# First matrix memory of a hybrid encoder layer: two of four key blocks turned by VectorE and DRAM, mask sums on VectorE, units in one written order

## The chip, the cores and the metric

The kernel runs on one core of one Trainium2 chip. The metric is the device time of one execution in microseconds (us); lower is better. A core has TensorE (PE: matmuls and turns, written to eight PSUM banks), VectorE (DVE), ScalarE (ACT), GpSimd (POOL) and SyncE (SP). DMAs are issued from queues of SP and POOL. Each engine works through its own list of instructions in order and waits on semaphores.

## The reference

One encoder layer over two sequences of 512 tokens, model width 1024: a half-step SwiGLU FFN, a mixing block, a second half-step FFN, a final norm. The mixing block runs grouped-query attention and a bidirectional matrix memory (mLSTM) side by side on one projection `w_in`. What the change touches is the memory: four heads of width 128, for each head and direction

```
D    = b[:, None] - b[None, :] + li[None, :]          # b: running sum of log forget gates, li: input gate
S_qk = (q @ k.T) * exp(D - m)                         # masked to the past (forward) or the future (backward)
h    = (S_qk @ v + ...) / max(|sum S_qk + ...|, exp(-m))
...
h = h_fwd + h_bwd                                     # then RMS norm per head, times head_norm
mem = sigmoid(o_pre) * h
...
merged = sigmoid(g_att) * (att @ w_up_att) + sigmoid(g_mlstm) * (mem @ w_up_mlstm)
x = x + merged @ w_out
```

All is float32.

## The kernel before, in words

Activations lie transposed, channels on partitions and 512 tokens along the row. A float32 product is made of three float32r products: each operand is split into a high part (ACT copy) and a low part (DVE subtraction; `split`, lines 733 and 734, and for weights lines 284 and 285). So a projection of 128 output channels from 1024 inputs is 24 matmuls of 512 columns, one from 512 inputs (the merges) is 12.

`mix(s, ...)` is the mixing block of sequence s. The two sequences' blocks are generators that are run in turns. Work is written as *units*, pairs of a weight load and its matmuls; `go` runs them with one unit's load ahead for s = 0 (two for s = 1). A weight used by both sequences is loaded and split in s = 0 and parked in DRAM (line 309), and only fetched again in s = 1. Units here: `mem_values` (four units of 24 matmuls), `mem_qk(h, j)` (queries or keys of a head), `att_gate(d)`, `mem_gate(d)` (24 matmuls each), `merge_att(d)`, `merge_mem(d)` (12 each).

The order of instructions on each engine is made by a planner: a list scheduler that goes by priority (the order in which things are written, shifted by `with shifted(n)`) and by a model of durations and landing times. `pin` puts an instruction behind the one written just before it on its engine; `mark(i, last)` pins only while `marks[0]` is true.

The memory of a head (`mem_head`, line 1299) makes for each of four query blocks i a 128 x 512 score product in PSUM (line 1309), decay weights by `exp` on ACT (line 1323) from two rows that DMA spreads over the partitions (`mem_rows`: line 1088, and line 1091 adds the mask), the product of both on DVE (line 1325), and joins both directions in one 128 x 512 tile `Ts[i][0]` (lines 1336 to 1339). Since the value product needs keys on partitions, every 128 x 128 block of it must be turned.

In s = 0 `mem_out` (line 1359) turns all four key blocks j on PE: four turns (line 1372) into a PSUM bank, a split, and three value matmuls into one bank (line 1381). Then come the square (line 1390), the gate product, block sums, the root and the norm (lines 1391 to 1399). The heads stand in the loop at line 1423; the planner is free to order the units around them.

In s = 1 no PE turns are made: `mem_blocks` turns 32 x 32 blocks on DVE (line 1347), `mem_send` writes them to DRAM through POOL's queue (line 1355), and `mem_out` fetches them whole (line 1368). Its units are written out in one order with pins (lines 1401 to 1422).

Row tiles of 128 x 512 come from pools: `t2` (eleven), `f2` (four). Weight buffers: four `w8`. PSUM: three banks `mm`, one `o`, two `s`, two `t`. `mg` holds the gate rows, 128 x 8 x 512; rows 4 to 7 hold the raw queries until attention has turned them, rows 6 and 7 then stand empty until `att_gate(6)` and `att_gate(7)`.

Of the kernel before, what the change touches and what calls it, by code (L numbers as in the profile page):

```python
# [8 lines left out]
F32 = mybir.dt.float32  # L9
# [3 lines left out]
ALU = mybir.AluOpType  # L13
# [13 lines left out]
def encoder(ctx, tc, I, outs):  # L27
# [32 lines left out]
    def T2(dtype=F32, tag="t2"):  # L60
        if tag in ("eb", "ac"):
            i = boxes[tag]
            boxes[tag] += 1
            return boxes["tile"][:, i % 4 + (4 if tag == "ac" else 0), :]
        if tag == "R":
            return spool.tile([P, S], dtype, tag="R", bufs=2, name=nm("R"))
        n = {"t2": 11, "f2": 4}[tag]
        return tpool.tile([P, S], dtype, tag=tag, bufs=n, name=nm(tag))
# [723 lines left out]
    def go(*units):  # L792
        for load, comp in units:
            held.append((comp, load()))
            while len(held) > ahead[0]:
                c, w = held.pop(0)
                c(w)
# [67 lines left out]
    def mix(s, xh, xl, early=None, extra=None, after=None):  # L865
# [5 lines left out]
        def fill(n):  # L871
            go(*queue[:n])
            del queue[:n]

        def F2(dtype=F32):
            return T2(dtype, "f2")
# [145 lines left out]
        def mem_values():  # L1022
            def done(pvv):
                vm = A([P, 2, 4, S], F32R, "Vm")
                for b in range(4):
                    nc.scalar.activation(vm[:, 0, b, :], pvv[b], AF.Copy, scale=rcol(b))
                    rest(vm[:, 1, b, :], pvv[b], b, f(vm[:, 0, b, :]))
                Vm.append(vm)
            return tok_proj(xh, xl, [(1792, 512)], 2, done, (MM, MM, MM, PO))
# [27 lines left out]
        def att_gate(d):  # L1057
            def done(pp):
                gate_of(mg[:, d, :], pp)
            return win_cols(2832 + d * P, done)  # L1060
# [23 lines left out]
        def mem_rows(h, d):  # L1084

            eb = T2(F32, "eb")
            eb3 = eb.rearrange("p (b s) -> p b s", b=4)
            nc.sync.dma_start(eb3, ebuf[d, :, h, :].partition_broadcast(P))
            em = T2(F32, "eb")
            em3 = em.rearrange("p (b s) -> p b s", b=4)  # L1090
            (V_ if s or not h else G_).tensor_tensor(em3, eb3, tabs[3][:, d].unsqueeze(1).to_broadcast([P, 4, P]), op=ALU.add)
            return eb3, em3

        def mem_scales():
# [178 lines left out]
        def merge_att(d):  # L1273
            def done(pu):
                V_.scalar_tensor_tensor(mg[:, d, :], mg[:, d, :], 1.0, pu, op0=ALU.add, op1=ALU.mult)
            return up_unit(0, d, att, done)
# [17 lines left out]
            return up_unit(1, d, mem, done, (PS, PT)[d % 2])  # L1294

        mem = A([P, HM, 2, S], F32R, "mem")
        own = [T2(F32, "R")] if s else []

        def mem_head(h):
            qk = qks[h]  # L1300
            ebs, ems = zip(*[mem_rows(h, d) for d in range(2)])
            dn_ = small(8, "dn")
            dn = dn_.rearrange("p (d b) -> p d b", d=2)
            Ts = []
            for i in range(4):
                p = PS()
                isl = slice(i * P, (i + 1) * P)
                for n, (a, b) in enumerate(((0, 2), (0, 3), (1, 2))):
                    nc.tensor.matmul(p, qk[a][:, isl], qk[b], start=(n == 0), stop=(n == 2))
                pair = []  # L1310
                for d in range(2):
                    W = T2()
                    st_ = i if d == 0 else 3 - i
                    for j in range(st_ + 1):
                        b = j if d == 0 else 3 - j
                        if j == st_:
                            src, bias = ems[d][:, j], bd[:, d, st_, h:h + 1]
                        else:
                            src = ebs[d][:, j]
                            dist = st_ - j  # L1320
                            bias = (n1[:, d, st_, h:h + 1] if dist == 1 else
                                    n2[:, d, st_, h:h + 1] if dist == 2 else n2[:, d, 1, h:h + 1])
                        nc.scalar.activation(W[:, b * P:(b + 1) * P], src, AF.Exp, bias=bias)
                    cl = slice(0, (i + 1) * P) if d == 0 else slice(i * P, S)
                    V_.scalar_tensor_tensor(W[:, cl], p[:, cl], DM ** -0.5, W[:, cl], op0=ALU.mult, op1=ALU.mult,
                                            accum_out=dn[:, d, st_:st_ + 1])
                    pair.append(W)
                Ts.append(pair)
            V_.scalar_tensor_tensor(dn_, dn_, -1.0, dn_, op0=ALU.mult, op1=ALU.max)
            V_.tensor_tensor(dn, dn, en[:, :, :, h], op=ALU.max)  # L1330
            V_.reciprocal(dn_, dn_)
            for i in range(4):
                tf, tb = Ts[i]
                rf, rb = dn[:, 0, i:i + 1], dn[:, 1, 3 - i:4 - i]
                lo_, di_, up_ = slice(0, (i + 1) * P), slice(i * P, (i + 1) * P), slice((i + 1) * P, S)
                nc.scalar.activation(tf[:, lo_], tf[:, lo_], AF.Copy, scale=rf)
                V_.scalar_tensor_tensor(tf[:, di_], tb[:, di_], rb, tf[:, di_], op0=ALU.mult, op1=ALU.add)
                if i < 3:
                    V_.tensor_scalar(tf[:, up_], tb[:, up_], rb, None, op0=ALU.mult)
            return Ts  # L1340
# [18 lines left out]
        def mem_out(h, Ts):  # L1359
            moved = isinstance(Ts, int)  # L1360
            vm = Vm[0]
            po = PO()
            hs_ = slice(h * P, (h + 1) * P)
            turned = []
            for j in range(4 + 1):
                if j < 4 and moved:
                    p = F2()
                    mark(nc.gpsimd.dma_start(p, tbuf[Ts][4 * j:4 * j + 4].rearrange("c r a x -> (c r) (a x)")), True)
                elif j < 4:
                    p = PT()  # L1370
                    for i in range(4):
                        nc.tensor.transpose(p[:, i * P:(i + 1) * P], Ts[i][0][:, j * P:(j + 1) * P], ident)
                if j < 4:
                    ph, pl = T2(F32R), T2(F32R)
                    split(p, ph, pl)
                    turned.append((j, ph, pl))
                if j >= 1:
                    t, ph, pl = turned.pop(0)
                    with shifted(15):
                        for n, (a, b) in enumerate(((0, ph), (1, ph), (0, pl))):  # L1380
                            mark(nc.tensor.matmul(po, vm[:, a, t, hs_], b, start=(t == 0 and n == 0),  # L1381
                                                  stop=(t == 3 and n == 2)), True)
            h2 = T2()
            og = ogs[h]
            if moved:
                rows_ = T2()
                nc.scalar.activation(rows_.rearrange("p (i a m) -> p i a m", i=4, a=4),
                                     po.rearrange("p (a i m) -> p i a m", i=4, a=4), AF.Copy)
                po = rows_
            nc.scalar.activation(h2, po, AF.Square)  # L1390
            V_.scalar_tensor_tensor(og, og, 1.0, po, op0=ALU.add, op1=ALU.mult)
            turned_ = own[0] if own else F2()
            row = block_sums(h2, turned_)
            with shifted(60):
                rh = block_rstd(row, DM)
            with shifted(160):
                Rh = spread_rows(rh, turned_)
                V_.scalar_tensor_tensor(og, og, hn[:, h:h + 1], Rh, op0=ALU.mult, op1=ALU.mult)
                split(og, mem[:, h, 0, :], mem[:, h, 1, :])

        if s:
# [18 lines left out]
            go(*[mem_gate(d) for d in range(EARLY)])  # L1420
            mem_out(3, at[3])
            marks[0] = False
        for h in range(HM if not s else 0):
            Ts = mem_head(h)
            if h == 0:
                go(*mem_values())
            queue.append(merge_att(2 * h))
            if h == 0:
                queue.append(merge_att(1))
            fill(1 + s)  # L1430
            mem_out(h, Ts)
            if h + 2 < HM:
                queue.extend([att_gate(h + 6), mem_qk(h + 2, 0), mem_qk(h + 2, 1)])
            if h:
                queue.append(merge_att(2 * h + 1))
            fill(99)

        mh, ml = A([P, KD, S], F32R, "mh"), A([P, KD, S], F32R, "ml")
        go(*[mem_gate(d) for d in range(EARLY * s, KD)])
        go(*[merge_mem(d) for d in range(KD)])  # L1440
        flush()
        yield None
# [553 lines left out]
```

## Time and profile before

| what | before |
|---|---|
| time, median of 3 runs | 2029.29 us (2028.79 to 2030.15) |
| profiled execution | 2029.24 us, span 2027.5 us |
| PE busy | 2015.1 us (99%) |
| DVE busy | 1592.6 us (79%) |
| ACT busy | 919.2 us (45%) |
| POOL busy | 249.7 us (12%) |
| granted clock of PE | 0.999 |

The span runs from the first to the last instruction; the time of the execution is 1.7 us longer. Busy time is that of the named engine. Names such as `pst<-ident,t` say what is written (a bank of pool `t`) from what (`ident` and a row tile). Three numbers with slashes are least, median and largest duration in ns. A bracket at the end of a row of the timeline is idle time of that engine just before it, and what ended it.

### The profile page before, as it was taken

To read this page: it belongs to the slowest core of one execution; us is meant where nothing else is said; L and a number is where in the kernel's file an instruction comes from. 1 tells how busy PE (TensorE), PEld (TensorE's weight loads), DVE (VectorE), ACT (ScalarE), POOL (GpSimd) and SP (SyncE) were. 2 spreads that over 40 slices of the span, in tenths; PEclk is the share of its full clock that TensorE was granted. 3 is DMA by queue.
4 is the path that set the end of the run, shared out by engine and by line. 5 is a ranking of instruction groups with operands and counts; after the bars stand their busy time and mean duration, and the time that the engine had idled before them with its cause. 6 is when DMAs were issued, how large, how long until landed. Compare 5 with 4: busy or idle time off the path is not lost.

```text
span 2027.5 us, 26874 instructions
## 1 busy us (share of the span) xinstructions
PE 2015.1 (99%) x9129; PEld 1661.4 (82%) x9129; DVE 1592.6 (79%) x2830; ACT 919.2 (45%) x1677; POOL 249.7 (12%) x313
## 2 busy tenths in 40 slices
PE   9999999999999999999999999999999999999998
PEld 7888888888888888788888878888888888888887
DVE  8989898896688788786566867377798988786797
ACT  7644444443224477653325655245444444442224
POOL 0243344201003000100120023011000000000001
PEclk9999999999999999999999999999999999999999
DMA  9778787799766766868657668867565655699753
GB/s 313 233 235 271 228 279 244 258 337 373 264 220 220 274 194 198 267 206 300 210 165 220 205 228 264 274 208 238 157 210 171 226 168 178 204 339 349 272 194 120
DMA packets 329546, 482.11 MB, mean 238 GB/s; under 512 B 23016, under 2 KB 196160, under 8 KB 328128
## 3 DMA queue, kind: packets, MB, share of 16 engines
q1 hardware_dynamic: 316352, 439.27, 64.9%
q0 software_dynamic: 12896, 40.86, 5.9%
q8 instruction: 72, 1.18, 0.2%
q14 instruction: 66, 0.54, 0.1%
q10 hardware_dynamic: 160, 0.27, 0.0%
HBM read 308.70 MB, written 171.61 MB: 237 GB/s over the span
## 4 chain that ended last, share of the span: by engine, by line
PE 94%; DVE 2%; DMA 2%; issue 1%; ACT 1%; SPq 0%; DVEq 0%; ACTq 0%
PE mm L856 16%; PE mm L380 11%; PE pso L380 11%; PE pst L380 11%; PE mm L650 9%; PE mm L842 5%; PE pss L380 5%; PE pss L650 4%; PE pst L650 4%; PE mm L821 3%; PE pso L650 3%; PE pss L1118 1%; PE pso L1165 1%; PE pso L1381 1%; PE pst L856 1%; PE pss L856 1%
## 5 line engine op out<-in xcount | busy, mean ns | idle before, releaser
L380 PE MATMUL pst<-xc,w 128*128 128x512 f32 x1056 | 253.8, 389 | 0.5 <-ACT t L415 0.5
L380 PEld LDWEIGHTS pst<-xc,w 128*128 128x128 f32 x1056 | 198.1, 188 | 42.0 <-ACT t L415 0.9
L380 PE MATMUL mm<-xc,w 128*128 128x512 f32 x972 | 229.8, 390 | 0.8 <-ACT t L388 0.8
L380 PEld LDWEIGHTS mm<-xc,w 128*128 128x128 f32 x972 | 181.8, 188 | 39.5 <-ACT t L388 1.9
L650 PE MATMUL mm<-rt,w 128*128 128x512 f32 x765 | 178.7, 389 | 0.0
L856 PE MATMUL mm<-xh,w 128*128 128x512 f32 x560 | 176.0, 391 | 0.0
L650 PEld LDWEIGHTS mm<-rt,w 128*128 128x128 f32 x765 | 143.5, 188 | 29.8
L338 ACT ACTIVATE w<-t 128x512 fp32r<-128x512 f32 x176 | 107.6, 628 | 130.7 <-issue 59.1
L339 DVE TENSOR_TENSOR w<-t,w 128x512 fp32r<-128x512 f32 x176 | 120.2, 701 | 31.7 <-ACT w L338 30.0
L380 PE MATMUL pso<-xc,f 128*128 128x512 f32 x528 | 127.1, 390 | 0.1
L380 PE MATMUL pss<-xc,w 128*128 128x512 f32 x528 | 126.8, 389 | 0.0
L380 PE MATMUL pso<-xc,w 128*128 128x512 f32 x528 | 126.8, 389 | 0.0
L856 PEld LDWEIGHTS mm<-xh,w 128*128 128x128 f32 x560 | 104.9, 188 | 21.8
L380 PEld LDWEIGHTS pso<-xc,f 128*128 128x128 f32 x528 | 98.9, 188 | 21.5 <-DVE t L419 1.1
L380 PEld LDWEIGHTS pss<-xc,w 128*128 128x128 f32 x528 | 99.1, 188 | 20.6
L380 PEld LDWEIGHTS pso<-xc,w 128*128 128x128 f32 x528 | 99.1, 188 | 20.6
L842 PE MATMUL mm<-xh,w 128*128 128x512 f32 x336 | 110.5, 395 | 0.0
L856 PE MATMUL mm<-xl,w 128*128 128x512 f32 x280 | 109.6, 391 | 0.0
L733 ACT ACTIVATE w<-wr 128x512 fp32r<-128x512 f32 x72 | 45.1, 632 | 138.3 <-PE pso L650 70.6
L733 ACT ACTIVATE w<-t 128x512 fp32r<-128x512 f32 x82 | 51.8, 632 | 107.4 <-PE pst L650 62.4
L650 PE MATMUL pss<-rt,w 128*128 128x512 f32 x396 | 93.7, 389 | 0.0
L650 PE MATMUL pst<-rt,w 128*128 128x512 f32 x396 | 93.7, 389 | 0.0
(464 smaller groups left out, 4168.1 us busy)
## 6 DMA issues: line engine op xcount, KB each, us to landing
rt<-rbuf SPq DMA_DIRECT2D x154, 512.0 KB, 5.8
w<-wpark SPq DMA_DIRECT2D x112, 512.0 KB, 5.1
wpark<-w SPq DMA_DIRECT2D x64, 512.0 KB, 3.6
wr<-in_ffn_w_gate_dram SPq DMA_DIRECT2D x62, 512.0 KB, 5.5
wr<-in_ffn_w_up_dram SPq DMA_DIRECT2D x44, 512.0 KB, 4.8
rbuf<-f SPq DMA_DIRECT2D x86, 256.0 KB, 4.3
rbuf<-R SPq DMA_DIRECT2D x82, 256.0 KB, 4.7
rbuf<-tab SPq DMA_DIRECT2D x74, 256.0 KB, 3.9
```

The source lines that it names most:

```text
L338: pin(nc.scalar.activation(t[:, 0], src, AF.Copy))
L339: pin(V_.tensor_tensor(t[:, 1], src, f(t[:, 0]), op=ALU.subtract))
L380: nc.tensor.matmul(p, a[:, k, :], xt[:, b, k, :], start=(first and k == 0 and i == 0), stop=(k == HK_ - 1 and i == 2), skip_group_check=True)
L650: nc.tensor.matmul(p, u[:, a, d * P:(d + 1) * P], r[:, b, ts], start=(first and q == 0 and k == 0), stop=(q == len(us) - 1 and k == 2), sk ...
L733: nc.scalar.activation(hi, src, AF.Copy)
L821: mark(nc.tensor.matmul(p[b][:, :N], a[:, k, bs], w_[:, kl, :], start=(k == 0 and i == 0), stop=(k == KD - 1 and i == 2)), (kl, b, i) == ( ...
L842: pin(nc.tensor.matmul(p[0], a[:, k, :], b, start=(k == 0 and i == 0), stop=(k == n - 1 and i == 2)))
L856: mark(nc.tensor.matmul(p, a[:, k, :], b, start=(k == 0 and i == 0), stop=last), last)
L1118: pin(nc.tensor.matmul(p, qT[:, h, b * P:(b + 1) * P], kv[:, hk * 2 + j, :], start=(j == 0), stop=(j == 1)))
L1165: pin(nc.tensor.matmul(pos[h], Vst[:, kb, h // 4, :], w, start=(kb == KBS[0] and i == 0), stop=(kb == KBS[3] and i == 1)))
L1381: mark(nc.tensor.matmul(po, vm[:, a, t, hs_], b, start=(t == 0 and n == 0), stop=(t == 3 and n == 2)), True)
```

## The change

In s = 0, key blocks 0 and 1 of each head are turned by DVE in 32 x 32 blocks (four instructions of 128 x 256 a head) into rows 6 and 7 of `mg`, sent to DRAM in four DMAs on POOL's queue and fetched back in two. Key blocks 2 and 3 are turned on PE as before, and now stand first in the value product. The value product's columns come in another order, so that an ACT copy puts them back (as in s = 1). The mask sums of heads 1 to 3 move from POOL to DVE. The units around the four heads are written out in one order, and the last matmul of each, the turns, the value matmuls and the DMAs are pinned; five of the `mem_gate` units are written among the heads, where before all eight stood behind them. The norm uses the copied row as its scratch row. The counts of matmuls, units and weight loads stay.

```
-            (V_ if s or not h else G_).tensor_tensor(em3, eb3, tabs[3][:, d]...)
+            V_.tensor_tensor(em3, eb3, tabs[3][:, d]...)
...
+        def half_send(h, Ts):
+            q = mg[:, 6:8].rearrange("p a (n i m) -> p (a n) i m", i=4, m=32)
+            for i in range(4):
+                V_.transpose(q[:, :, i, :], Ts[i][0][:, 0:256].rearrange("p (n m) -> p n m", m=32))
+            for a in range(4):
+                mark(nc.gpsimd.dma_start(tbuf[h % 2][0:8, :, a, :].rearrange("n r x -> r n x"),
+                                         q[32 * a:32 * a + 32].rearrange("r n i m -> r n (i m)")), True)
+        def half_turns(h, Ts):
+            got = []
+            for j in (2, 3):
+                p = PT()
+                for i in range(4):
+                    mark(nc.tensor.transpose(p[:, i * P:(i + 1) * P], Ts[i][0][:, j * P:(j + 1) * P], ident), True)
+                got.append((j, *parts(p.rearrange("p (i a m) -> p a i m", i=4, a=4))))
+            return got
+        def half_values(h, po, got):
+            for t, ph, pl in got:
+                for n, (a, b) in enumerate(((0, ph), (1, ph), (0, pl))):
+                    mark(nc.tensor.matmul(po, Vm[0][:, a, t, h * P:(h + 1) * P], b, ...), True)
+        def half_rest(h):
+            got = []
+            for j in range(2):
+                p = F2()
+                mark(nc.gpsimd.dma_start(p, tbuf[h % 2][4 * j:4 * j + 4].rearrange("c r a x -> (c r) (a x)")), True)
+                got.append((j, *parts(p)))
+            return got
+        def half_norm(h, po):
...
-        for h in range(HM if not s else 0):
-            Ts = mem_head(h)
-            if h == 0:
-                go(*mem_values())
-            queue.append(merge_att(2 * h))
-            if h == 0:
-                queue.append(merge_att(1))
-            fill(1 + s)
-            mem_out(h, Ts)
-            if h + 2 < HM:
-                queue.extend([att_gate(h + 6), mem_qk(h + 2, 0), mem_qk(h + 2, 1)])
-            if h:
-                queue.append(merge_att(2 * h + 1))
-            fill(99)
+        else:
+            qk2, qk3 = [[mem_qk(h, j) for j in range(2)] for h in (2, 3)]
+            ma = [merge_att(d) for d in range(KD)]
+            mgs = [mem_gate(d) for d in range(KD)]
+            marks[0] = True
+            for h, (first, one, more) in enumerate((
+                    ([*mem_values(), qk2[0]], qk2[1], [ma[0], ma[1], ma[2]]),
+                    ([ma[3], qk3[0], qk3[1]], ma[4], [ma[5], mgs[0]]),
+                    ([mgs[1]], mgs[2], [att_gate(6)]),
+                    ([att_gate(7), ma[6]], ma[7], [mgs[3], mgs[4]]))):
+                Ts = mem_head(h)
+                half_send(h, Ts)
+                go(*first)
+                got = half_turns(h, Ts)
+                go(one)
+                po = PO()
+                half_values(h, po, got)
+                go(*more)
+                half_values(h, po, half_rest(h))
+                half_norm(h, po)
+            marks[0] = False
...
-        go(*[mem_gate(d) for d in range(EARLY * s, KD)])
+        go(*([mem_gate(d) for d in range(EARLY, KD)] if s else mgs[5:]))
```

Since `go` runs one unit behind, the last unit of each list computes at the start of the next list.

More of the change, by code (lines that the diff above doesn't have):

```diff
@@ L1090, in mem_rows @@
             em3 = em.rearrange("p (b s) -> p b s", b=4)
-            (V_ if s or not h else G_).tensor_tensor(em3, eb3, tabs[3][:, d].unsqueeze(1).to_broadcast([P, 4, P]), op=ALU.add)
+            V_.tensor_tensor(em3, eb3, tabs[3][:, d].unsqueeze(1).to_broadcast([P, 4, P]), op=ALU.add)
             return eb3, em3
@@ L1296, in mix @@
         mem = A([P, HM, 2, S], F32R, "mem")
-        own = [T2(F32, "R")] if s else []
+        own = T2(F32, "R") if s else None
         def mem_head(h):
@@ L1391, in mem_out @@
             V_.scalar_tensor_tensor(og, og, 1.0, po, op0=ALU.add, op1=ALU.mult)
-            turned_ = own[0] if own else F2()
+            turned_ = own if s else po
+            row = block_sums(h2, turned_)
+            with shifted(60):
+                rh = block_rstd(row, DM)
+            with shifted(160):
+                Rh = spread_rows(rh, turned_)
+                V_.scalar_tensor_tensor(og, og, hn[:, h:h + 1], Rh, op0=ALU.mult, op1=ALU.mult)
+                split(og, mem[:, h, 0, :], mem[:, h, 1, :])
@@ new lines, in half_values @@
+        def half_values(h, po, got):
+            for t, ph, pl in got:
+                for n, (a, b) in enumerate(((0, ph), (1, ph), (0, pl))):
+                    mark(nc.tensor.matmul(po, Vm[0][:, a, t, h * P:(h + 1) * P], b, start=(t == 2 and n == 0),
+                                          stop=(t == 1 and n == 2)), True)
+        def half_rest(h):
[5 more added lines that the diff above has]
+            return got
@@ new lines, in half_norm @@
+        def half_norm(h, po):
+            h2 = T2()
+            og = ogs[h]
+            if True:
+                rows_ = T2()
+                nc.scalar.activation(rows_.rearrange("p (i a m) -> p i a m", i=4, a=4),
+                                     po.rearrange("p (a i m) -> p i a m", i=4, a=4), AF.Copy)
+                po = rows_
+            nc.scalar.activation(h2, po, AF.Square)
+            V_.scalar_tensor_tensor(og, og, 1.0, po, op0=ALU.add, op1=ALU.mult)
+            turned_ = own if s else po
```

## Prediction

> **What bounds the kernel now.** I read the engine shares first, then the busy time by stage, then the chain of waits inside the stage that the change touches.
>
> ```profile
> span 2027.5 us, 26874 instructions
> ...
> PE 2015.1 (99%) x9129; PEld 1661.4 (82%) x9129; DVE 1592.6 (79%) x2830; ACT 919.2 (45%) x1677; POOL 249.7 (12%) x313
> ```
>
> TensorE (PE) is busy for 2015.1 of 2027.5 us, so time is won only by giving PE less to do or by closing its few gaps. The stages, with columns PE, PEld, DVE, ACT, POOL, granted clock, DMA share and GB/s:
>
> ```profile
> 797.00:960.00 163.00, 161.90 (x750) 131.20 (x749) 122.06 (x271) 89.65 (x182) 8.66 (x7) 1.00 0.75 253
> 960.00:1160.00 200.00, 200.00 (x962) 166.52 (x962) 138.13 (x290) 93.55 (x187) 28.48 (x42) 1.00 0.62 195
> 1160.00:1300.00 140.00, 139.26 (x617) 112.78 (x616) 89.69 (x257) 66.31 (x161) 29.45 (x52) 1.00 0.78 259
> ```
>
> The first row holds the first matrix memory (s = 0), the last row the second one (s = 1), which already turns all its blocks through VectorE (DVE) and DRAM. PE idles 1.10 us in the first and 0.74 us in the second. Next, the operation that the change halves, and two rows of the chain of waits that price it:
>
> ```profile
> L1372 PE MATMUL pst<-ident,t x64: 270/272/328, 828.3 to 916.2; 128*128 128x128 f32 x64
> ...
> 828.50 0.87 PE pst L1372 x8
> ...
> 834.27 5.89 PE mm L856 x26
> ```
>
> All 64 turns of L1372 lie in s = 0 (16 a head). One is in flight for 272 ns, but on the chain, where matmuls overlap, eight take 0.87 us: 0.109 us each. A 512-column matmul takes 5.89/26 = 0.227 us there. The 1.10 us of idle time are these two gaps (the bracket is idle time and its releaser):
>
> ```profile
> 812.54 0.97 PE L1309 MATMUL pss<-qk 128*128 128x512 f32 x3 [0.70 <-DVE t L1325]
> ...
> 854.72 0.93 PE L1309 MATMUL pss<-qk 128*128 128x512 f32 x3 [0.40 <-DVE t L1325]
> ```
>
> **The change part by part.**
>
> *Half of the PE turns go.* Four heads lose 8 turns each: 32 × 0.109 = **3.5 us** off the chain. PE gets nothing new: units, scores and value matmuls are the same, in another order. The Trainium skill ("TensorE: Matmul & The Clock Gate", Part 4: PE-mode transpose) puts a turn at about 275 ns in a kernel's context. By that the term would be 8.8 us; the trace has that duration in flight, but 0.109 us a turn on the chain, and I take the chain.
>
> *Block turns on DVE, sends and fetches on GpSimd's queue (POOL).* The prices stand in s = 1:
>
> ```profile
> L1347 DVE STREAM_TRANSPOSE qt<-t x32: 407/411/444, 1191.0 to 1261.9; 128x256 f32<-128x256 f32 x32
> 1239.86 2.73 DVE L1347 STREAM_TRANSPOSE qt<-t 128x256 f32<-128x256 f32 x8
> L1355 POOL DMA_DIRECT2D tbuf<-qt x32: 582/585/618, 1194.2 to 1266.3; - x32
> DMA to landing us min/median/max: 3.8/5.9/7.1
> 1242.56 4.64 POOL L1355 DMA_DIRECT2D tbuf<-qt  x8 [17.50 <-DVE qt L1347]
> 1248.70 1.12 POOL L1368 DMA_DIRECT2D f<-tbuf  x2 [1.50 <-DMA tbuf<-qt]
> L1368 POOL DMA_DIRECT2D f<-tbuf x16: 537/546/572, 1203.0 to 1272.6; - x16
> DMA to landing us min/median/max: 3.0/5.8/9.1
> L1387 ACT ACTIVATE t<-pso x4: 597/598/601, 1225.9 to 1297.1; 128x512 f32<-128x512 f32 x4
> ```
>
> DVE: 16 turns × 2.73/8 = 5.5 us. ScalarE (ACT): four row copies as at L1387, 4 × 0.60 = 2.4 us. POOL: 16 sends × 0.585 and 8 fetches × 0.546 = 13.7 us. DMA: 16 × 128 KB and 8 × 256 KB, some 4 MB beside the 253 GB/s × 163 us = 41 MB that the stage moves, share 0.75 to about 0.83. The splits of the two fetched blocks cost as before, but read SBUF instead of PSUM (ACT 622 for 596 ns, DVE 691 both times):
>
> ```profile
> L733 ACT ACTIVATE t<-pst x50: 575/596/602, 726.3 to 1171.9; 128x512 fp32r<-128x512 f32 x50
> L733 ACT ACTIVATE t<-f x46: 615/622/633, 730.9 to 1294.6; 128x512 fp32r<-128x512 f32 x46
> L734 DVE TENSOR_TENSOR t<-pst,t x50: 652/691/694, 727.0 to 1172.6; 128x512 fp32r<-128x512 f32 x50
> L734 DVE TENSOR_TENSOR t<-f,t x46: 659/691/701, 731.6 to 1295.5; 128x512 fp32r<-128x512 f32 x46
> ```
>
> *The six mask sums of heads 1 to 3 move from POOL to DVE.*
>
> ```profile
> L1091 POOL TENSOR_TENSOR box<-box,tab x6: 1285/1294/1734, 819.3 to 880.6; 128x512 f32<-128x512 f32 x6
> L1091 DVE TENSOR_TENSOR box<-box,tab x1: 684/684/684, 803.3 to 803.3; 128x512 f32<-128x512 f32 x1
> ...
> 849.97 3.04 POOL L1091 TENSOR_TENSOR box<-box,tab 128x512 f32<-128x512 f32 x2 [13.33 <-DMA box<-ebuf]
> 852.12 1.98 DVE L285 TENSOR_TENSOR w<-wr,w 128x1024 fp32r<-128x1024 f32 x1
> 856.78 1.23 DVE L285 TENSOR_TENSOR w<-wr,w 128x1024 fp32r<-128x1024 f32 x1
> ```
>
> DVE gains 6 × 0.68 = 4.1 us and POOL loses 7.7 us. But DVE pays already: while POOL ran two sums at 849.97, a weight split on DVE took 1.98 instead of 1.23 us. It ran just ahead of the 0.40 us gap at 854.72; with these sums on DVE I count that gap closed, **0.4 us** (0 to 0.4). The 0.70 us at 812.54 belongs to head 0, whose sums were on DVE already: it stays. DVE ends at 122.06 + 5.5 + 4.1 = 132 of 163 us, ACT at 92: neither becomes the bound on average.
>
> *The wait that is new.* The value matmuls of the two fetched blocks are pinned behind the units written before them, and can go only when the data are back. From the last finished score row: four turns 1.4 us; four sends until the first fetch may go 6.1 (1242.56 to 1248.70); the second fetch's issue 0.55; its landing 5.8 (3.0 to 9.1); split on ACT and DVE 0.62 + 0.69. Sum 15.2 us (12.4 to 18.5). On PE, between a head's own turns and those matmuls, in units of 24 matmuls (5.4 us) or 12 (2.7 us):
> - head 0: 8 turns 0.9, qk 5.4, six value matmuls 1.4, qk 5.4, two merges 5.4: 18.5 us;
> - heads 1 and 2: 0.9 + 5.4 + 1.4 + 5.4 = 13.1 us, and 2.7 more where the next head's scores slip in;
> - head 3: 0.9 + 2.7 + 1.4 + 2.7 + 5.4 = 13.1 us.
>
> So head 0 is covered and the others are short by 2.1 us if their scores are finished only when the turns start. How far ahead they are is read from head 2 of before:
>
> ```profile
> 882.39 1.36 PE pss L1309 x6
> ...
> 893.28 0.68 PE pst L1372 x6
> ```
>
> A head's scores take 10.9 us to be ready. Heads 1 and 3 have 10.9 us of units and 2.7 us of scores ahead of their turns, so they are about 2.7 us early, and that pays for the 2.1. Head 2 has one gate unit, 8.2 us with the scores: 2.7 us late, unless its scores start under head 1's last units. Unpinned matmuls of later units can fill such holes, as far as three PSUM banks and the weight buffers reach. Lower end 0; upper end three heads at 5.4 us (18.5 - 13.1) plus 2.7: 19 us. The nearest row is the 0.74 us of the whole s = 1 stage, but with longer cover; I take **1.3 us**. The Trainium skill ("DMA: Bandwidth & Descriptors", Anatomy of one DMA) gives about 2.0 us + bytes/436e3 for a DMA of this kind. An estimate by it is 2.3 us for a send, 2.6 us for a fetch, and no wait at all; the landings measured here are 5.9 and 5.8 us, and they decide.
>
> *Queues.* The send and fetch are in written order on POOL. A fetch that waits 6 us holds up only the next head's sends, which come later anyway; without the mask sums nothing else stands there. The six sums now wait for their DMA in DVE's queue, and the fetched blocks' splits in ACT's. What such a wait costs s = 1 (us in total, times, longest):
>
> ```profile
> DVE box L1091 <- DMA box<-ebuf: 5.9, 3, 2.9
> ACT t L733 <- DMA f<-abuf: 5.3, 1, 5.3
> ...
> 851.01 1.05 ACT L284 ACTIVATE w<-wr 128x1024 fp32r<-128x1024 f32 x1
> 919.50 0.60 ACT L1390 ACTIVATE t<-pso 128x512 f32<-128x512 f32 x1 [2.05 <-PE pso L1381]
> 928.98 0.63 ACT L733 ACTIVATE mem<-box 128x512 fp32r<-128x512 f32 x1 [3.44 <-DVE box L1398]
> ```
>
> Behind them stand weight splits (L284: 1.05 us on ACT, L285: 1.23 us on DVE a unit). A unit's weights are split while the unit before runs, 5.4 us, so 5.4 - 2.3 = 3.1 us are spare; waits of up to 2.9 us are hidden, one of 5.3 us costs PE 2.2 us. That lies in the bounds above. SP's loads and parked stores follow the units' order at unchanged count: nothing. Gate rows 6 and 7 hold the turned blocks until head 3's sends are read, so att_gate(6)'s result stays in its PSUM bank some 8 us longer; two banks held, the third serves the merge: hidden. Five mem gates come earlier and hold five of eleven row tiles; the last four, 21.8 us, still hide head 3's norm, about 10 us (919.50 to 929.61, the last two rows).
>
> **The sum.** -3.5 - 0.4 + 1.3 = -2.6 us. The profiled execution took 2029.24 us around its span of 2027.5 (1.7 us outside), 0.05 us under the median of 2029.29. So 2029.24 - 2.6 = **2026.6 us**, a change of 0.13%.
>
> **The rivals.**
> - *Clean cover:* no new wait, and the small waits of values on split turns shrink too. For it: head 0 is fully covered, and unpinned units can fill. Against: 13.1 us against 15.2. Time: 2029.24 - 3.5 - 1.1 = 2024.6, 2023.5 with the transitions.
> - *A turn is worth its whole 272 ns:* 32 × 0.272 = 8.7 us, 2020.5 us. Against: eight in 0.87 us. The skill's Part 4 stands beside this one.
> - *The gain is eaten:* two heads short by 2.1 us each (4.2), or one stalled split (2.2) and one head: 2029.24 - 3.9 + 4.2 = 2029.5 us; up to 2033 with three. The change then takes turns off PE as it says, and gives the time back as waits at the value matmuls.
> - *Slower:* the round trip through DRAM at its long end, 18.5 us, in heads 1 to 3. Each is then 5.4 us short, less what slips in (2.7 in two): 10.8 us; 2029.24 - 3.9 + 10.8 = 2036 us. It decides from 2.7 us a head on (3 × 2.7 = 8.0 = 3.9 + 4.1). For it: the DMA share goes above 0.8, landings reached 9.1 us. Against: unpinned work for the holes.
>
> **How the numbers follow.** 0.2% of 2029 is 4.06 us, about what a measurement can tell from no change: under 2025.2 is faster, over 2033.3 slower. Chances: forecast (2025.2 to 2028.5) 48%, clean cover 20%, a full 272 ns 2%, eaten (2028.5 to 2033.3) 18%, slower 12%. Faster 0.22, same 0.66, slower 0.12. The range from 2023.5 to 2032.3 leaves out the 272 ns case, most of the slower case and the edge of the eaten one.
>
> **What the profile after would show.** Right: L1372's 64 turns gone, 32 in their place; 16 more block turns on DVE; no mask sum on POOL; PE idle in the stage near 2 us; the stage some 3 us shorter with everything behind it shifted. Wrong: value matmuls of blocks 0 and 1 idling on a split or on the fetch, a weight split late behind a waiting ACT or DVE, or a merge waiting for a bank held by the gate rows.

## The result, and the profile after

| what | before | after |
|---|---|---|
| median of 5 runs each, same chip | 2029.29 us (2028.58 to 2031.49) | 2048.78 us (2047.93 to 2050.12) |
| ratio, 95% interval | | 1.0094 (1.008 to 1.0109) |
| span of the profiled execution | 2027.5 us | 2046.3 us |

The change costs 19.5 us, 0.96%. The forecast of 2026.6 us missed on size and on sign, and the range ended at 2032.3. The page of the changed kernel, its span and engine shares:

```profile
span 2046.3 us, 26875 instructions
...
PE 2018.2 (99%) x9097; PEld 1662.3 (81%) x9097; DVE 1597.9 (78%) x2852; ACT 922.6 (45%) x1681; POOL 256.0 (13%) x331
```

The span grew by 18.8 us, and two subtractions split that. PE's idle time went from 2027.5 - 2015.1 = 12.4 to 2046.3 - 2018.2 = 28.1 us: **15.7 us more waiting**. Its busy time went up by 3.1 us although 32 turns are gone (9129 to 9097 instructions), which should have taken off 3.5: so the matmuls that are left took about **6.6 us more** (an estimate, as the 3.5 us are the prediction's term). Both lie in the stage of the first matrix memory (columns as before: PE, PEld, DVE, ACT, POOL, granted clock, DMA share, GB/s):

```profile
797.00:960.00 163.00, 145.86 (x622) 115.48 (x621) 113.10 (x266) 84.63 (x173) 13.89 (x24) 0.93 0.76 248
```

PE is busy for 145.86 of 163 us, where it was 161.90; the granted clock is 0.93, where it was 1.00. What PE waited for there (total, times, longest, in us), and the waits in PE's timeline:

```profile
PE pst L1415 <- DVE t L1339: 6.6, 1, 6.6
PE pso L1422 <- ACT t L733: 4.9, 2, 3.2
PE mm L856 <- DVE mg L889: 3.4, 1, 3.4
```
```profile
877.62 1.22 PE L1422 MATMUL pso<-t,Vm 128*128 128x512 f32 x2 [3.21 <-ACT t L733]
...
914.69 0.73 PE L1422 MATMUL pso<-t,Vm 128*128 128x512 f32 x2 [1.65 <-ACT t L733]
...
931.37 0.74 PE L1415 MATMUL pst<-ident,t 128*128 128x128 f32 x2 [6.64 <-DVE t L1339]
932.94 1.54 PE L1415 MATMUL pst<-ident,t 128*128 128x128 f32 x6 [0.83 <-DVE t L1337]
934.32 2.93 PE L1422 MATMUL pso<-t,Vm 128*128 128x512 f32 x6
940.61 5.14 PE L856 MATMUL mm<-att,w 128*128 128x512 f32 x12 [3.37 <-DVE mg L889]
```

Three kinds of wait are new. L1422 waits for the split of a fetched block (heads 1 and 2). The first turns of head 3 (L1415; L1372 in the kernel before) wait 6.64 us for its score rows, not for its own trip through DRAM. A merge (L856) waits 3.37 us for a bank that the multiplication of a gate result (L889) still holds. The granted clock falls at the long ones; each row gives its mean over 5 us:

```profile
875.00:880.00 5.00, 2.38 (x6) 1.90 (x7) 2.40 (x4) 2.10 (x3) 0.00 (x0) 0.70 0.75 265
880.00:885.00 5.00, 5.00 (x16) 3.91 (x15) 0.78 (x3) 0.76 (x2) 0.00 (x0) 0.62 0.79 261
...
915.00:920.00 5.00, 5.00 (x23) 3.94 (x21) 3.02 (x7) 3.13 (x9) 0.00 (x0) 1.00 0.93 317
...
930.00:935.00 5.00, 2.80 (x10) 2.01 (x10) 4.79 (x16) 3.00 (x6) 0.55 (x1) 0.50 1.03 313
935.00:940.00 5.00, 2.25 (x6) 1.28 (x4) 0.83 (x2) 0.12 (x1) 1.81 (x4) 0.50 0.69 205
940.00:945.00 5.00, 4.39 (x10) 3.47 (x11) 3.17 (x5) 1.23 (x2) 1.12 (x2) 0.50 0.36 108
```

Behind the gap of 3.21 us a matmul takes 0.43 us (the chain below, 878.84); in stretches of 2.5 us the clock is 0.50 from 877.5 to 882.5. The second slow stretch begins within the gap of 6.64 us and stays at 0.50 from 930 to 945. The gap of 3.37 us lies inside it, and the twelve merge matmuls behind that gap take 5.14 us, where the prediction counted 2.7. The gap of 1.65 us leaves the clock at 1.00.

Why the waits arise shows in two views. First the chain of waits, cut to the turns and the round trip of head 1 and to the passage from head 2 to head 3:

```profile
861.11 0.23 DVE t L1337
861.34 1.02 DVE mg L1405 x3
...
862.65 1.35 POOL tbuf L1407 x3
...
864.41 5.12 DMA tbuf<-mg
...
870.16 6.76 DMA f<-tbuf
876.94 0.64 ACT t L733
877.62 1.22 PE pso L1422 x2
878.84 0.43 PE pss L1309
...
917.30 0.61 ACT t L1438
917.96 0.50 issue
918.47 2.19 ACT t L1323 x8
```

From the end of the last score row (861.11 + 0.23 = 861.34) to the value matmul at 877.62 the round trip takes 16.3 us; the prediction had 15.2. At the passage from head 2 to head 3, head 3's first decay weights (L1323) run straight behind head 2's copy (L1438) and square (L1441). ACT's timeline shows this for heads 1 and 3:

```profile
848.51 0.63 ACT L1441 ACTIVATE t<-t 128x512 f32<-128x512 f32 x1
849.04 5.07 ACT L1323 ACTIVATE t<-box,st 128x128 f32<-128x128 f32 x17
...
917.93 0.63 ACT L1441 ACTIVATE t<-t 128x512 f32<-128x512 f32 x1
918.47 5.66 ACT L1323 ACTIVATE t<-box,st 128x128 f32<-128x128 f32 x19
...
928.90 0.40 ACT L1323 ACTIVATE t<-box,st 128x128 f32<-128x128 f32 x1 [2.88 <-DVE box L1449]
```

L1441 is the square in a head's norm, behind its last value matmul. Head 3 needs twenty weights, and the last of them waits until L1449, the last multiplication of head 2's norm, is done. No input of a weight comes from there. That the norm's copied row, read by L1449, holds the row tile which the last weight needs fits both the trace and the program, but no run isolates it.

So a head's decay weights begin only when the head before has its fetched blocks back, and at head 3 the last one waits for the whole norm. (Two of head 3's four score products were made on PE earlier, at 904.27; they had to wait for their weights.) The hypothesis from this: neither the round trip nor the order of the heads costs anything alone, but **in series** a head needs its weights and scores, then the trip, then the copy, and only then the next head's weights start. The units that PE has for one head are shorter than that chain.

### The profile page after: what moved, and what is told of

It reads as the page before. It is cut to its first block, busy times and chain, and to the rows that moved or that the text cites. A ratio compares the mean times of both kernels' runs of the same rounds, so it can differ in the third digit from the quotient of the medians.

```text
span 2046.3 us, 26875 instructions
## 1 busy us (share of the span) xinstructions
PE 2018.2 (99%) x9097; PEld 1662.3 (81%) x9097; DVE 1597.9 (78%) x2852; ACT 922.6 (45%) x1681; POOL 256.0 (13%) x331
## 4 chain that ended last, share of the span: by engine, by line
PE 92%; DMA 3%; DVE 2%; ACT 2%; issue 1%; POOL 0%; SPq 0%; DVEq 0%; ACTq 0%; POOLq 0%
PE mm L856 14%; PE pso L380 12%; PE pst L380 11%; PE mm L380 10%; PE mm L650 8%; PE pss L380 6%; PE mm L842 5%; PE pss L650 4%; PE pst L650 4%; PE mm L821 3%; PE pso L650 3%; PE pss L1118 1%; PE pso L1165 1%; PE pst L856 1%; PE pss L856 1%; PE pso L821 1%
## 5 line engine op out<-in xcount | busy, mean ns | idle before, releaser
L856 PE MATMUL mm<-xh,w 128*128 128x512 f32 x560 | 177.5, 392 | 0.0
L856 PEld LDWEIGHTS mm<-xh,w 128*128 128x128 f32 x560 | 105.4, 188 | 22.1
L856 PE MATMUL mm<-xl,w 128*128 128x512 f32 x280 | 109.8, 392 | 0.0
```

Source lines behind the costliest of these rows:

```text
L856: mark(nc.tensor.matmul(p, a[:, k, :], b, start=(k == 0 and i == 0), stop=last), last)
```

## The experiments

Each ran beside runs of the kernel before on the same chip; ratios are to those.

**Written order without the trip** (`pe_turns`). All four blocks are turned on PE; order, pins and DVE's mask sums are those of after.

```
-                half_send(h, Ts)
                 go(*first)
...
-                half_values(h, po, half_rest(h))
+                half_values(h, po, half_turns(h, Ts, (0, 1)))
```

> Keeps the changed kernel's written order, pins and DVE mask sums, but turns all four key blocks on PE; blocks 0 and 1 are turned where the fetch stood. No block turns, sends or fetches in s = 0. Theory A (serial heads: a head's scores start only behind the norm of the head before, so turns and values of each head come late in the written order, and the round trip makes that chain longer): the waits at the value matmuls (3.2 and 1.7 us) and at the bank of the gate rows (3.4 us) go, the wait of head 3's turns for its scores (6.6 us) shrinks but stays at 2 to 6 us: 2031 to 2038 us. Rival B (the round trip through DRAM alone is the loss): all gaps go, 2028 to 2031 us. Rival C (pins and written order alone are the loss): 2043 us or more.

Measured: 2030.0 us, ratio 1.0005 (0.9995 to 1.0015), so in the range of 2028 to 2031 (the trip as the whole loss), and the range of 2031 to 2038 fell. Its stage, and its ACT timeline at the last head:

```profile
797.00:960.00 163.00, 161.72 (x745) 130.37 (x744) 120.72 (x276) 90.52 (x184) 0.00 (x0) 1.00 0.74 253
```
```profile
905.89 0.63 ACT L1441 ACTIVATE t<-t 128x512 f32<-128x512 f32 x1
906.43 5.65 ACT L1323 ACTIVATE t<-box,st 128x128 f32<-128x128 f32 x19
```

The decay weights still start right behind the square, the twentieth comes only at 918.46, and yet head 3's wait of 6.64 us is gone. PE had work there: rows 6 and 7 are free in this kernel, the two gate results are written at 912.05 and 918.05, and 22 of the 24 matmuls of merges 6 and 7 run from 917.29 until head 3's first turns at 922.28. The order alone is not the loss.

**The next head's scores ahead of the fetched values** (`early`). The round trip stays as it is.

```
+            Ts = mem_head(0)
             for h, (first, one, more) in enumerate((...)):
-                Ts = mem_head(h)
                 half_send(h, Ts)
...
                 half_values(h, po, got)
+                if h + 1 < HM:
+                    Ts = mem_head(h + 1)
                 go(*more)
                 half_values(h, po, half_rest(h))
```

> The changed kernel with one move: the scores of head h+1 are written ahead of the last units of head h, so ahead of its fetched blocks' value matmuls and its norm. Round trip, pins and units as they are. Theory A: decay weights of the next head are made during the round trip, head 3's turns no longer wait for scores, and most of the gaps go: 2026 to 2034 us. Rival B: the round trip is untouched, 2043 us or more. Rival C: pins untouched, 2043 us or more.

Measured: 2027.13 us, ratio 0.9991 (0.9982 to 1.0001): the loss is gone with the DRAM trip in place. Its stage, PE's largest wait there, and the decay weights of head 3 beside the square of head 2:

```profile
797.00:960.00 163.00, 160.17 (x722) 128.76 (x721) 128.44 (x294) 93.53 (x188) 15.16 (x25) 1.00 0.83 279
```
```profile
PE pso L1422 <- DVE t L734: 1.2, 1, 1.2
```
```profile
894.70 5.95 ACT L1323 ACTIVATE t<-box,st 128x128 f32<-128x128 f32 x20
...
909.85 0.63 ACT L1441 ACTIVATE t<-t 128x512 f32<-128x512 f32 x1
```

Head 3's weights stand 15 us ahead of the square, not behind it. All twenty stand in one row, with no wait for a norm. With `pe_turns` this shows the cause: trip and serial order are a loss only together; either one taken away brings the time back. (`pe_early` below takes both away: 2027.81 us.)

**Pins off** (`no_pins`). The written order stays; the marks that hold instructions to it are off.

```
-            marks[0] = True
+            marks[0] = False
```

> The changed kernel with marks off in s = 0: same written order, same round trip, the planner may place value matmuls, turns, sends and fetches. Theory A: the chain from head to head stays, since what starts a head's scores is not a pin; 2038 to 2050 us. Rival C (pins): back to 2025 to 2031 us. Rival B: 2045 to 2052 us.

Measured: 2047.18 us, ratio 1.009 (1.0075 to 1.0105), with the same three waits (6.6, 5.3 and 3.3 us in total). The range for pins as the loss, 2025 to 2031 us, fell; the other two ranges overlap here, so the run does not choose between them. The order holds without the pins, so it comes from the sequence in which the work is written.

**Gate units 6 and 7 later** (`gates_later`). Other units take their place, so that nothing has to write rows 6 and 7 while the turned blocks stand there.

```
-                    ([mgs[1]], mgs[2], [att_gate(6)]),
-                    ([att_gate(7), ma[6]], ma[7], [mgs[3], mgs[4]]))):
+                    ([mgs[1]], mgs[2], [mgs[3]]),
+                    ([mgs[4], mgs[5]], att_gate(6), [att_gate(7), ma[6], ma[7]]))):
...
-        go(*(... if s else mgs[5:]))
+        go(*(... if s else mgs[6:]))
```

> The changed kernel with the units of heads 2 and 3 in another written order: mem_gate(3) to (5) come first, att_gate(6), att_gate(7) and merge_att(6), (7) stand behind head 3's turns, so that nothing waits for rows 6 and 7 of the gate tile while head 3's sends read them. Theory A: the 3.4 us wait goes, the wait for head 3's scores stays or grows: 2041 to 2047 us. Rival D (the gate rows are the main loss): 2034 us or less.

Measured: 2041.62 us, ratio 1.0059 (1.0044 to 1.0074). Its page and its waits in the stage:

```profile
span 2039.2 us, 26873 instructions
...
PE 2014.4 (99%) x9097; PEld 1660.0 (81%) x9097; DVE 1597.4 (78%) x2852; ACT 923.3 (45%) x1681; POOL 257.8 (13%) x331
```
```profile
PE pst L1415 <- DVE t L1339: 5.5, 1, 5.5
PE pso L1422 <- ACT t L733: 5.5, 2, 3.4
```

The wait for the bank of a gate row is gone and the other two stay. Against after the span is 7.1 us shorter: 3.3 us of idle time (28.1 to 24.8) and 3.8 us of busy time. So this order is worth about 7 us of the 19, more than half of it (3.8 us) because PE's matmuls took less time. The edit also puts one more gate unit, `mem_gate(5)`, among the heads, so how much of the 7 us belongs to the held rows alone is not separated.

**Turned blocks in a tile of their own** (`own_rows`). This was to test the same thing by another way: a weight buffer takes the place of rows 6 and 7.

```
-            q = mg[:, 6:8].rearrange("p a (n i m) -> p (a n) i m", i=4, m=32)
+            q = wpool.tile([P, 8, 4, 32], F32, tag="wr", bufs=4, name=nm("qt"))
```

> The changed kernel with the turned blocks in a weight buffer (one of four wr) in place of rows 6 and 7 of the gate tile. Theory A: only the wait of a merge for a bank held by the gate rows (3.4 us, and the low clock before it) goes: 2042 to 2047 us. Rival D (the gate rows are the main loss): 2034 us or less. A raw weight buffer less may cost something.

Measured: 2080.25 us, ratio 1.0252 (1.0237 to 1.0268), a miss. PE now waits for weights, here from 790 to 1000 us of this longer run:

```profile
PE mm L856 <- ACT w L284: 20.8, 3, 9.8
```

The buffer that I took was one that the weights need. The run says nothing on the gate rows.

**Idle gaps filled with idle matmuls** (`filled`). 59 matmuls whose result nobody reads stand where the three gaps were, to keep the clock up at unchanged waits.

```
+                if h == 3:
+                    spare(30)
                 got = half_turns(h, Ts)
...
+                if h == 3:
+                    spare(15)
                 go(*more)
+                rest_ = half_rest(h)
+                if h == 1:
+                    spare(14)
...
```

> The changed kernel with 59 idle matmuls (512 columns, result unused) put on PE where it sat waiting: 14 ahead of head 1's fetched blocks, 30 ahead of head 3's turns, 15 behind head 3's first value matmuls. They shorten no wait; they only keep PE at work during it. Theory A with the clock as a second term (after the gaps of 3.2 and 6.6 us the matmuls that follow take 0.43 instead of 0.227 us): the granted clock of the stage returns to about 1.0 and 4 to 8 us are won, 2041 to 2045 us. Without the clock as a term: 2048 to 2052 us.

Measured: 2049.88 us, ratio 1.0097 (1.008 to 1.0114). That misses the 2041 to 2045 us and lies in the 2048 to 2052 us expected if the clock were no term. Its longest waits in the stage:

```profile
PE pso L1422 <- ACT t L733: 5.3, 1, 5.3
PE mm L856 <- DVE mg L889: 1.9, 1, 1.9
```

The stage's clock rose from 0.93 to 0.98, but head 2's values now wait 5.3 us in one piece where it was 1.65, with slow matmuls behind it. The filling did not hold the other waits fixed, so the run is no clean test of either range, and what the clock costs by itself stays open; 6.6 us is the accounting above, not an isolated result.

**Mask sums back on POOL** (`pool_sums`), and **mask sums on DVE in the kernel before** (`before_dve_sums`): the same line, both ways.

```
-            V_.tensor_tensor(em3, eb3, ...)
+            (V_ if s or not h else G_).tensor_tensor(em3, eb3, ...)
```

> The changed kernel with the mask sums of heads 1 to 3 back on POOL. Theory A: they stand early in each chain and cost it 1.3 instead of 0.7 us and some queueing behind POOL's DMAs: 2048 to 2053 us. Rival E (the sums on DVE are a loss of their own): 2045 us or less.

Measured: 2052.6 us, ratio 1.0113 (1.0098 to 1.0129), in the range of 2048 to 2053. In the profiled execution, the longest of four with 2056.27 us, the wait for the bank grows from 3.4 to 5.9 us, and that for fetched blocks from 4.9 to 7.8:

```profile
PE mm L856 <- DVE mg L889: 5.9, 1, 5.9
```

This points to some 4 us that the move to DVE saves in the changed kernel; the two intervals overlap.

> The kernel before with one line of the change: the six mask sums on DVE. By the prediction's term: the 0.40 us gap ahead of head 1's scores closes, 2028.3 to 2029.3 us for a kernel before at 2029.3. Rival E: slower by 1 us or more.

Measured: 2028.0 us, ratio 0.9993 (0.9983 to 1.0002). All that is left of PE's waits in the stage:

```profile
PE pss L1309 <- DVE t L1325: 0.7, 1, 0.7
```

The kernel before ran at 2030.06 us beside it, so the time lies under the range, but the interval includes no change; the rival (slower by 1 us or more) fell. The 0.40 us gap at 854.72 is closed, as the prediction counted; so small a term cannot be told in the time.

**What the trip is worth once nothing waits** (`pe_early`), **and both repairs together** (`early_gates`). The first is the early order with all blocks turned on PE, the second is the early order with the later gate units.

```
+                got = half_turns(h, Ts, (0, 1))
                 if h + 1 < HM:
                     Ts = mem_head(h + 1)
                 go(*more)
-                half_values(h, po, half_rest(h))
+                half_values(h, po, got)
```

> The early order with all four blocks turned on PE (blocks 0 and 1 turned ahead of the next head's scores), no DMA for them: what the DRAM trip itself is worth once nothing waits for it. Theory A (32 turns are worth their 3.5 us on the chain): 3.5 us less the waits that the trip leaves, about 1 to 3 us above the early order: 2028 to 2030.5 us, ratio 0.9995 to 1.0015, stage PE busy 162 to 163. Rival B (the order alone won those microseconds, and the trip through DRAM is worth nothing): 2026 to 2027.5 us, equal to the early order or below it.

> The early order (next head's scores written ahead of this head's fetched values and norm), and in it the later order of the gate units 6 and 7. Theory A (the two causes, serial heads and gate rows held, are separate, and the early order left the second partly open): 2024.5 to 2026.5 us, ratio 0.997 to 0.9985, PE idle in the stage under 2.0 us. Rival B (with the heads early, the rows are read out in time anyway): as the early order alone, 2026.5 to 2028 us, PE idle in the stage 2.5 to 3.2 us, no wait for a bank in either.

`pe_early`: 2027.81 us, ratio 0.9994 (0.9986 to 1.0003), between the two ranges, so the time does not decide what the trip is worth. PE's busy time speaks for the price of a turn, by the pages of `pe_early` and of `early`:

```profile
PE 2013.7 (99%) x9129; PEld 1661.8 (82%) x9129; DVE 1595.9 (79%) x2836; ACT 920.9 (45%) x1681; POOL 238.2 (12%) x307
```
```profile
PE 2010.2 (99%) x9097; PEld 1657.8 (82%) x9097; DVE 1598.4 (79%) x2852; ACT 921.3 (45%) x1681; POOL 257.1 (13%) x331
```

At the same order of units, 32 turns fewer make PE 3.5 us less busy, 0.109 us a turn. That it comes out to the tenth is luck: each is one execution, and the four profiled kernels with all 64 turns range from 2013.7 to 2015.1 us. The busy time also does not reach the time of the kernel: PE idles 2.8 us in the stage in `early` and 1.0 us in `pe_early`, and the two ratios (0.9991 and 0.9994) have overlapping intervals.

`early_gates`: 2026.38 us, ratio 0.9985 (0.9976 to 0.9994): 3.0 us faster than before by the medians, and by the ratios about 22 us faster than the changed kernel. PE's waits in its stage:

```profile
PE pss L1309 <- DVE t L1325: 0.9, 2, 0.7
PE pso L1422 <- DVE t L734: 0.8, 1, 0.8
PE mm L821 <- ACT w L284: 0.3, 1, 0.3
```

Its interval overlaps that of `early`, and PE waits 2.0 us here against 2.8 there. The time lies in theory A's range (2024.5 to 2026.5), the idle time in the stage, 2.06 us, just above its 2.0; that the gate order still brings something in the early order is not settled.

## Why the prediction was wrong

The first point rests on two rows of the kernel before, ACT's decay weights for head 2, and the second on a row of the changed kernel, DVE's gate results for rows 6 and 7:

```profile
867.48 4.19 ACT L1323 ACTIVATE t<-box,st 128x128 f32<-128x128 f32 x14
...
873.05 1.86 ACT L1323 ACTIVATE t<-box,st 128x128 f32<-128x128 f32 x6
```
```profile
939.86 1.29 DVE L889 TENSOR_TENSOR mg<-mm,R 128x512 f32<-128x512 f32 x2 [4.02 <-DMA tbuf<-mg]
```

- **"A head's scores take 10.9 us to be ready ... Heads 1 and 3 ... are about 2.7 us early": the step that failed.** The 10.9 us start at head 2's score matmuls (882.39), when its decay weights had long been made (867.48 to 874.91). The weights and the norm of the head before, behind which they start, were left out. At head 1 the chain from head 0's last value matmul (ends at 847.84) to the last score row (861.34) took 13.5 us, so head 1 was not early at all. Its cover was the 13.1 us that the prediction counted, the trip 16.3, and the difference is the wait of 3.21 us. At head 3 it took 14.1 us from head 2's copy (917.30) to the first turn (931.37). The kernel before starts its weights behind the square too, but no trip stands in its loop, so its profile never charged for that. The prediction asked what waits for the trip and not what waits for the one who waits.
- **"Gate rows ... hidden": failed.** The merge waited 3.37 us for a bank, the sign named for a wrong prediction. The results of `att_gate(6)` and `att_gate(7)` could be written only at 939.86, when head 3's sends had read the rows, and merge 6 needs gate row 6 as well (L1275 at 941.25). So all three `mm` banks were held from 924.7 on, and nothing behind them could fill head 3's 6.64 us. In `pe_turns`, with the rows free, merges 6 and 7 did run in that place. The order in `gates_later` brought 7 us, with one unit more among the heads.
- **"Unpinned matmuls of later units can fill such holes": they did, once.** Head 2's turns came late, as forecast, and PE did not idle: it ran 54 matmuls of gate units between 882.48 and 897.62, where the prediction counted one unit of 24. But that work was taken from head 3. The prediction counted 13.6 us of units and scores ahead of head 3's turns; from 917.3 to 924.7, some 7.4 us, was left. With the pins off (`no_pins`) the hole stayed. In `gates_later` 5.52 us of it stay, and the next unit there waits for a bank too (0.31 us, L889); what held that bank was not isolated.
- **The round trip itself was sized well:** 16.3 us at head 1 and 14.8 at head 2 against 15.2, and the waits for fetched blocks are 3.21 + 1.65 = 4.9 us, near the 4.2 us of the rival "The gain is eaten". The excess at head 1 lies in the sends: from the first send to the fetch 870.16 - 862.65 = 7.5 us, not 6.1 (a row that held eight sends, not four). The trip's size alone could not have moved the result.
- **The clock was left out of every price.** Waits were added as microseconds of idle time, but two slow stretches, behind the 3.21 us and around the 6.64 and 3.37 us, also slowed the matmuls there, some 6.6 us in sum by the accounting above. The Trainium skill ("TensorE: Matmul & The Clock Gate", Why this matters for your kernels) warns of idle gaps over about 3 us between matmul bursts, after which the clock falls to half. This trace agrees: 0.50 behind 3.21 and 6.64 us, 1.00 behind 1.65 us.
- **The "slower" rival** had the right sign but the wrong mechanism: it put the loss on a long round trip in each head. The trip was 16.3 us, not 18.5, and the waits at head 3 were for its scores and for a bank. Its 2036 us was still 13 us short.
- **Right:** a turn's price of 0.109 us (PE's busy time in `pe_early` against `early`, with the reserve given there); the 0.40 us gap closed by the sums on DVE; neither DVE nor ACT became the bound (128.44 and 93.53 of 163 us busy in `early`, forecast 132 and 92). Where scores and trip are not in series, the medians are 1.1 us below the kernel before in `early` and 3.0 us in `early_gates`. The forecast of -2.6 us lies between, but both are other orders of work, so this does not confirm its sum.

## What to carry to other kernels

When a latency is put into a loop that is written one pass after the other, add up the whole chain of a pass, from its first input to the place behind which the next pass may start, and compare that with the work that PE has for one pass; cover behind the wait alone is not enough. The repair costs nothing in instructions: start the next pass ahead of the wait. And count a PE gap as long as those here (3.21 and 6.64 us) at more than its length, because of the slower matmuls behind it. Work that may move forward fills a hole only once: ask what is left for the next one, and whether a bank is free for it.

## What the runs showed that I had not expected

- The slow clock outlasts its gap: behind 3.21 us matmuls took 0.43 us until about 884, some 6 us later; around the 6.64 and 3.37 us gaps the clock stood at 0.50 from 930 to 945 without a break. The other order of gate units in `gates_later` won 3.8 us of busy time beside 3.3 us of idle time.
- Work given to PE to bridge a gap did not help: 59 idle matmuls raised the stage's clock from 0.93 to 0.98, and the time stayed at 2049.88 us.
